# The opening of a hybrid attention layer: two tiles of x taken alone, a fixed order, and later copies

## The chip, the cores and the metric

The kernel runs on one core of one Trainium2 chip. The metric is the device time of one execution in microseconds, the median of several runs. Names used below: PE is TensorE (matmuls and transposes), DVE is VectorE, ACT is ScalarE, POOL is GpSimd, SP is the engine whose queue issues most transfers (DMAs).

## The reference

One decoder layer on x of 1024 positions by 1024 columns, in float32:

```python
def hybrid_layer(x, ...):
    h = rms_norm(x, pre_g)
    z = jnp.einsum('bsd,de->bse', h, w_in)            # 1024 x 7184 columns of weights
    qa, ka, va, ga, qb, kb, vb, gb, gk_low = split_columns(z)
    oa = diff_attention(qa, ka, va, lam)              # 8 heads, two softmax maps each, causal
    oa = rms_norm(oa, subln_g) * (1.0 - lam_init) * silu(ga)
    gk = gk_low @ w_gk_up + b_gk
    ob = gla_chunked(qb, kb, vb, log_sigmoid(gk) / 16)  # 4 heads of gated linear attention
    ob = rms_norm(ob, gla_g) * silu(gb)
    y = concatenate([oa, ob]) @ w_out
    return x + rms_norm(y, post_g)

def rms_norm(x, g):
    y = x * rsqrt(mean(x * x, axis=-1) + 1e-6)
    return y * g
```

## The kernel before

**Tiles.** x is eight tiles of 128 positions. Each is loaded, normed (`norm_x`: ScalarE squares and sums a tile, `rstd` makes the reciprocal root out of small ScalarE and VectorE steps, `scale_x` multiplies the tile by it), and turned by TensorE transposes (`tr`), 128 by 128 at a time, into PSUM banks. There are eight banks, handed out and taken back in turn by `take_bank` and `free`.

**High and low parts.** A float32 product is made of three matmuls of a faster 32-bit type: each operand is split into a rounded high part and the rest, the low part. ScalarE makes high parts, VectorE low parts: `put` for turned x (with the norm's gain `pre_g`), `make_weights` for weights (L315 and L316), `parts` for sums.

**Seven products.** The big product x by w_in is done in the Strassen-Winograd way: x and each block of weights (a "pair", 256 columns) are cut into two by two blocks, and seven products with sums of blocks replace eight. `order` lists the steps as (pair, product); one step is 24 matmuls of 256 columns for a wide pair (VA, VB), 12 of 512 for others. Products 1 and 2 need only h11 and h12, blocks of x's first four tiles; product 4 needs h22, and 5, 6, 7 and 3 need the sums s1, s2, s3 and s4. `blocks(j)` turns a quarter of the other four tiles, splits h22 and makes s1, s2 and s3; s4 is made afterwards (L625 and L627). A wide pair with an odd number uses the same weights as the even one before it, on the other two tiles of the half: in `multiply` the even pair reads tiles 0 and 1 of a half, the odd one tiles 2 and 3.

**The opening.** x's tiles 0 to 3 are loaded, then pre_g, the weights of pair 0, x's tiles 4 to 7, and more weights. `norm_x` runs for tiles 0 to 3, `first(0)` turns the first half of the columns of all four (16 transposes) and splits it into h11, step 0 runs, `first(1)` makes h12, two steps run, tiles 4 to 7 are normed, one more step runs, and then four times `blocks(j)` and a step; two steps follow, and s4.

**What sets the order.** All matmuls and transposes stay in program order (`mm` and `tr`). For the rest a scheduler lists each engine's instructions ahead of time by a simulated timeline, in program order where it can, and moves ready work ahead. `tc.keep_in_program_order` pins an instruction among the pinned ones of its engine; `tc.issue_after` puts one behind another. On the chip each engine then takes its list strictly in order. `prepare(i)` makes the weights of step i, `go(n)` runs n steps and prepares three steps ahead; weights come from buffers (`raw`, four of 512 KB) filled through SP's queue, and split weights lie in a ring of five buffers (`NRING`).

```python
        for st in range(1, NT - 1):
            part, nxt = nxt, mix(st + 1)
            rows = slice(ENDS[st - 1] * P, ENDS[st - 1] * P + P)
            sp.dma_start(out[0, rows, :], x[0, rows, :])
```

These lines, in `out_early` late in the program, copy six tiles of x to the output, onto which the result is added at the end. Nothing holds them back, so in the scheduler's list they stand early in SP's queue.

Of the kernel before, what the change touches and what calls it, by code (L numbers as in the profile page):

```python
# [14 lines left out]
P = 128  # L15
# [16 lines left out]
def hymba_kernel(  # L32
# [21 lines left out]
    act, dve, pool, pe, sp = nc.scalar, nc.vector, nc.gpsimd, nc.tensor, nc.sync  # L54
# [145 lines left out]
    order = [(0, 1), (1, 1), (0, 2), (1, 2), (2, 1), (3, 1), (2, 2), (3, 2), (4, 1), (4, 2)]  # L200
# [21 lines left out]
    LEAD = 8  # L222
    ws, ws_wide, early = {}, {}, {}

    def load_early(p):

        c0 = pairs[p][2]
        if wide(p):
# [4 lines left out]
        for kh, r in enumerate(early[p]):  # L233
            rows = slice(kh * 512, kh * 512 + 512)
            n = 256 if wide(p) else P
            sp.dma_start(r, w_in[0, rows, c0 : c0 + n].rearrange("(k p) c -> p k c", p=P))

    def prepare(i):

        if i >= len(order) or i in ws:  # L240
            return
        if i < 4:

            act_ins, dve_ins = normed[0][:2]
            with tc.issue_after(act_ins.ins), tc.issue_after(dve_ins.ins):
                make_weights(i)
        else:
            make_weights(i)
# [171 lines left out]
    def step(i):  # L420
# [22 lines left out]
        if n == 1:  # L443
            snap("s1", ps)
        elif n == 2:
            done(0, 0, ps, b["s1"])
            free.append(b["iy"])
        elif n == 6:
            snap("s2", ps)
        elif n == 7:  # L450
            snap("s3", ps)
            free.append(b["ix"])
            done(1, 1, b["z"], b["s3"])
            done(1, 0, b["y"], b["s3"])
            free.append(b["iy"])
        elif n == 3:
            done(0, 1, ps, b["s2"])
            free.append(b["iz"])
# [25 lines left out]
    norms, normed = {}, []  # L484

    def norm_x(*sts):
        n = len(sts)
        ssq = const.tile([P, 4, n], F32, tag=f"ssq{sts[0]}", name="ssq", bufs=1)
        for i, st in enumerate(sts):
            junk = hw.tile([P, D], F32, tag=("s2_hi0", "s2_lo0")[st % 2], name="junk")  # L490
            ins = act.activation(
                junk, xs[st], AF.Square, scale=D**-0.5, accum_out=ssq[:, 0, i : i + 1]
            )
            if n == 1:
                tc.keep_in_program_order(ins)
        pin = tc.keep_in_program_order if n == 1 else None
        normed[:] = [rstd(nc, ssq[:, :, :n], ssq[:, 0, :n], eps_t, pin)]
        for i, st in enumerate(sts):
            norms[st] = ssq[:, 1, i : i + 1]
            if n == 1:  # L500
                pin(scale_x(st, cols(0), dve))
# [10 lines left out]
    load_early(2)  # L512
    load_early(4)
    for st in range(4):
        norm_x(st)
    for st in range(4):
        scale_x(st, cols(1))

    def put(ps, k, dst, j):
        hi, lo = dst  # L520
        act.activation(at(hi, j), ps, AF.Copy, scale=pre_g[:, k : k + 1])
        dve.scalar_tensor_tensor(
            at(lo, j), ps, pre_g[:, k : k + 1], fp(at(hi, j)), ALU.mult, ALU.subtract
        )
# [4 lines left out]
    def first(h):  # L529

        ps = [take_bank([P, 512], "xT") for _ in range(HB)]
        for i in range(4):
            for j in range(HB):
                k = h * HB + j
                tr(ps[j][0][:, i * P : (i + 1) * P], xs[i][:, k * P : (k + 1) * P])
        hi, lo = H[("h11", "h12")[h]]
        for j in range(HB):
            put(ps[j][0], h * HB + j, (hi, lo), j)
            if h:
                act.activation(f1[h][:, j], ps[j][0], AF.Copy, scale=pre_g[:, h * HB + j : h * HB + j + 1])  # L540
            else:
                pool.tensor_tensor(f1[h][:, j], fp(at(hi, j)), fp(at(lo, j)), ALU.add)
# [51 lines left out]

    def go(n):
        for _ in range(n):
            i = made[0]
            if i == len(order):
# [23 lines left out]
    go(2)  # L622
# [89 lines left out]
    sp.dma_start(bgk, b_gk[0].rearrange("(t p) -> p t", p=P))  # L712
# [7 lines left out]
    sp.dma_start(sub_g, attn_subln_g[0].rearrange("(p o) -> p o", o=1))  # L720
    dve.tensor_scalar(sub_g, sub_g, 1.0 - LAM_INIT, None, ALU.mult)
    sp.dma_start(gla_g, gla_norm_g[0].rearrange("(t p) -> p t", p=P))
# [536 lines left out]
    def out_early():  # L1259
# [109 lines left out]
    LAST, ENDS = 2, [4, 5, 6, 7, 0, 1, 2, 3]  # L1369
# [156 lines left out]
```

## Time and profile before

| what | value |
|---|---|
| median of 3 runs | 979.72 us (978.95 to 979.96) |
| the profiled execution | 979.08 us, of which the span is 977.4 |
| granted TensorE clock, mean | 0.999 |
| busy: PE, DVE, ACT, POOL | 98%, 75%, 61%, 15% |
| first transpose, first product | 7.21 us, 14.41 us |

The span runs from the first instruction to the last; what lies around it is in the execution's time and not in the profile. A row of the timeline gives start, duration, engine, line, operation, tiles written and read, shapes and count; in brackets stands how long the engine was idle before it and what released it.

### The profile page before, as it was taken

The numbers are of one execution on the slowest core, as the hardware profiler recorded it, in microseconds if no ns is written. First come the engines' busy times: TensorE is split into PE (matmuls) and PEld (weight loads), VectorE is DVE, ScalarE is ACT, GpSimd is POOL, SyncE is SP. The second block draws the span as 40 slices with busy tenths as digits, with TensorE's granted clock in tenths as the row PEclk, the third lists the DMA queues.
The fourth block names the chain that finished last, engine by engine and source line by source line (L and its number), as shares of the span: only waits on it lengthen the run. The fifth ranks groups of instructions, "written<-read, shape, count | busy, mean of one in ns | idle before, by whom it ended". The sixth has DMA issues, their size and how long they took to land.

```text
span 977.4 us, 15766 instructions
## 1 busy us (share of the span) xinstructions
PE 956.7 (98%) x5338; PEld 830.4 (85%) x5338; DVE 735.4 (75%) x1452; ACT 600.5 (61%) x1164; POOL 142.9 (15%) x158
## 2 busy tenths in 40 slices
PE   5999999999999999999999999999999999999997
PEld 5998988888889998999888888878888888888785
DVE  6887597789866667686786876487888888898554
ACT  8742455487357455454665775366776687887773
POOL 4300000000000010000200002121322222443321
PEclk9999999999999999999999999999999999999999
DMA  9432446656774868897987866987656669994677
GB/s 345 151 110 91 139 135 205 231 179 225 238 247 162 264 187 286 254 294 229 293 259 243 273 202 191 407 269 272 197 186 228 240 199 344 340 294 105 151 208 147
DMA packets 152593, 220.45 MB, mean 226 GB/s; under 512 B 17104, under 2 KB 83664, under 8 KB 152416
## 3 DMA queue, kind: packets, MB, share of 16 engines
q1 hardware_dynamic: 146176, 203.71, 64.1%
q0 software_dynamic: 6336, 15.73, 7.0%
q8 instruction: 42, 0.69, 0.3%
q14 instruction: 39, 0.32, 0.1%
HBM read 133.93 MB, written 88.60 MB: 228 GB/s over the span
## 4 chain that ended last, share of the span: by engine, by line
PE 95%; DVE 2%; ACT 1%; DMA 1%; issue 1%; POOL 0%; SPq 0%; DVEq 0%; ACTq 0%; POOLq 0%
PE x L117 24%; PE y L117 15%; PE z L117 15%; PE ypart L117 13%; PE sc L117 7%; PE po L117 5%; PE yps L117 4%; PE wtr L120 3%; PE gpo L117 3%; PE kv L117 1%; PE gkl_ps L117 1%; PE pa L117 1%; DMA x<-in_x_dram 1%; PE xT L120 1%; DVE s_lo L548 0%
## 5 line engine op out<-in xcount | busy, mean ns | idle before, releaser
L315 ACT CAST w<-w_raw 128x512 fp32r<-128x512 f32 (+1 forms) x164 | 112.4, 688 | 94.7 <-PE y L117 44.1
L316 DVE TENSOR_TENSOR w<-w_raw,w 128x512 fp32r<-128x512 f32 (+1 forms) x164 | 126.7, 774 | 50.1 <-ACT w L315 43.3
L1049 ACT ACTIVATE p<-p,stt 128x896 f32<-128x896 f32 (+7 forms) x128 | 99.3, 777 | 36.7 <-DVE stt L1039 33.9
L427 ACT COPY s<-x 128x512 f32<-128x512 f32 x84 | 49.1, 585 | 84.4 <-PE x L117 84.3
L775 POOL TENSOR_SCALAR_AFFINE_SELECT gan<-gan 128x512 f32<-128x512 f32 x8 | 16.5, 2060 | 485.4 <-ACT gan L774 449.8
L296 DVE TENSOR_TENSOR w_raw<-w_raw 128x512 f32<-128x512 f32 (+1 forms) x96 | 75.9, 791 | 13.9 <-DMA w_raw<-in_w_in_dram 12.6
L1039 DVE CUSTOM_DVE_ANT_0 p<-sc,maskt 128x512 f32<-128x512 f32 (+3 forms) x128 | 74.3, 585 | 14.5 <-PE sc L117 13.3
L117 PE MATMUL ypart<-wo_hi,m_hi 128*128 128x512 f32 x192 | 79.5, 414 | 0.1
L117 PE MATMUL y<-h_hi,w 128*128 128x512 f32 x320 | 79.6, 391 | 0.0
L117 PE MATMUL z<-s_hi,w 128*128 128x512 f32 x320 | 79.6, 391 | 0.0
L117 PE MATMUL x<-s_hi,w 128*128 128x512 f32 x320 | 79.6, 391 | 0.0
L1055 POOL TENSOR_SCALAR p<-p,stt,lam 128x1024 f32<-128x1024 f32 (+3 forms) x64 | 56.2, 879 | 146.9 <-DVE stt L1054 141.9
L117 PE MATMUL ypart<-wo_hi,m_lo 128*128 128x512 f32 x192 | 75.5, 393 | 0.0
L117 PE MATMUL ypart<-wo_lo,m_hi 128*128 128x512 f32 x192 | 75.4, 393 | 0.0
L117 PE MATMUL sc<-k,q 128*128 128x512 f32 (+1 forms) x192 | 69.0, 363 | 1.3 <-DVE stt L1039 1.2
L117 PEld LDWEIGHTS x<-s_hi,w 128*128 128x128 f32 x320 | 59.7, 188 | 12.2
L117 PEld LDWEIGHTS y<-h_hi,w 128*128 128x128 f32 x320 | 59.6, 188 | 12.2
L117 PEld LDWEIGHTS z<-s_hi,w 128*128 128x128 f32 x320 | 59.5, 188 | 12.0
L117 PE MATMUL sc<-ks,q 128*128 128x512 f32 (+1 forms) x192 | 66.1, 347 | 0.0
L1097 ACT CAST wt_hi<-wtr 128x512 fp32r<-128x512 f32 (+1 forms) x80 | 42.7, 534 | 24.6 <-PE wtr L120 23.8
L1098 DVE TENSOR_TENSOR wt_lo<-wtr,wt_hi 128x512 fp32r<-128x512 f32 (+1 forms) x80 | 50.7, 633 | 8.6 <-ACT wt_hi L1097 8.0
L1058 DVE SCALAR_TENSOR_TENSOR p<-p,stt,p 128x1024 f32<-128x1024 f32 (+3 forms) x64 | 52.1, 814 | 4.1 <-POOL p L1055 3.9
(226 smaller groups left out, 2247.7 us busy)
## 6 DMA issues: line engine op xcount, KB each, us to landing
w_raw<-in_w_in_dram SPq DMA_DIRECT2D x56, 512.0 KB, 4.7
wo_raw<-in_w_out_dram SPq DMA_DIRECT2D x32, 256.0 KB, 3.0
wo_d<-wo_hi SPq DMA_DIRECT2D x32, 256.0 KB, 2.8
wo_d<-wo_raw SPq DMA_DIRECT2D x32, 256.0 KB, 3.8
q<-q_d SPq DMA_DIRECT2D x32, 256.0 KB, 4.7
k<-k_d SPq DMA_DIRECT2D x32, 256.0 KB, 5.7
ks<-k_d SPq DMA_DIRECT2D x64, 128.0 KB, 6.2
v<-v_d SPq DMA_DIRECT2D x16, 512.0 KB, 7.0
```

What stands on the lines that cost most here:

```text
L117: tc.keep_in_program_order(pe.matmul(*a, **k))
L120: tc.keep_in_program_order(pe.transpose(dst, src, ident))
L296: dve.tensor_tensor(dst, a, b, ALU.subtract)
L315: act.copy(w[0], src)
L316: dve.tensor_tensor(w[1], src, fp(w[0]), ALU.subtract)
L427: act.copy(b[k], ps)
L1039: ins = dve.tensor_tensor_reduce(p[:, a:e], sc[:, : e - a], maskt[:, NZ + P - (e - a) :] if last else maskt[:, : e - a], 1.0, 3e38 if i == ...
L1049: act.activation(p[:, :n], p[:, :n], AF.Exp, bias=st[:, m : m + 1], scale=-1.0, accum_out=st[:, 2 + m : 3 + m],)
L1055: pool.tensor_scalar(p1[:, :n], p1[:, :n], st[:, 5:6], lam, ALU.mult, ALU.mult)
L1058: dve.scalar_tensor_tensor(p0[:, :n], p0[:, :n], st[:, 4:5], p1[:, :n], ALU.mult, ALU.subtract)
L1097: act.copy(hi[:, :n], pt[:, :n])
L1098: dve.tensor_tensor(lo[:, :n], pt[:, :n], fp(hi[:, :n]), ALU.subtract)
```

## The change

- An engine wrapper (`Queue`) pins every ScalarE, VectorE and POOL instruction in program order while `pinned` is set, which holds from the first norm to the end of the first six steps.
- Transfers are issued as x tiles 0 and 1, the first half of pair 0's weights, pre_g, the first half of pair 2's weights, x tiles 2 and 3, the other halves, x tiles 4 to 7, and more weights.
- Tiles 0 and 1 are normed, turned and split alone (`first_tiles(0)`, half as wide); steps 0 and 1 are now (0,1) and (2,1), which read only these. Then tiles 2 and 3 follow (`first_tiles(2)`), step 2 (1,1), the second half of the columns of all four (`second_half`), step 3 (3,1), and two more steps, and only then the four rounds of `blocks(j)` and a step. The two steps behind the rounds are gone: they stand ahead of them.
- The squares of tiles 3, 5 and 7 are made by VectorE (`tensor_tensor_reduce`), not ScalarE. POOL scales the second half of the columns of tiles 0 to 3, and all of tiles 4 to 7, as before.
- The weights of step (0,5) are made behind the last pinned VectorE instruction.
- The six copies of x to the output are pinned in SP's queue at steps 20, 24, 28, 32, 36 and 40; the small loads bgk, sub_g and gla_g, and the scaling of sub_g, are pinned where the program has them.

```diff
-    act, dve, pool, pe, sp = nc.scalar, nc.vector, nc.gpsimd, nc.tensor, nc.sync
+    pe, sp = nc.tensor, nc.sync
+    pinned = [False]
+    class Queue:
...
+            def run(*a, **k):
+                ins = op(*a, **k)
+                if pinned[0]:
+                    tc.keep_in_program_order(ins)
+                    self.last = ins
+                return ins
...
+    act, dve, pool = Queue(nc.scalar), Queue(nc.vector), Queue(nc.gpsimd)
...
-    order = [(0, 1), (1, 1), (0, 2), (1, 2), (2, 1), (3, 1), (2, 2), (3, 2), (4, 1), (4, 2)]
+    order = [(0, 1), (2, 1), (1, 1), (3, 1), (0, 2), (1, 2), (2, 2), (3, 2), (4, 1), (4, 2)]
...
+    COPIES = range(20, 44, 4)
...
-        if i < 4:
-
-            act_ins, dve_ins = normed[0][:2]
-            with tc.issue_after(act_ins.ins), tc.issue_after(dve_ins.ins):
-                make_weights(i)
-        else:
+        with tc.issue_after(dve.last.ins) if order[i] == (0, 5) else nullcontext():
             make_weights(i)
...
+            if st in by_dve:
+                dve.tensor_tensor_reduce(
+                    junk, xs[st], xs[st], 1.0 / D, 0.0, ALU.mult, ALU.add, ssq[:, 0, i : i + 1]
+                )
+            else:
+                act.activation(
+                    junk, xs[st], AF.Square, scale=D**-0.5, accum_out=ssq[:, 0, i : i + 1]
+                )
...
-    for st in range(4):
+    for st in range(2):
         load_x(st)
+    load_raw(0, (0,))
     sp.dma_start(pre_g, pre_norm_g[0].rearrange("(k p) -> p k", p=P))
-    load_raw(0)
+    load_early(2, (0,))
+    for st in range(2, 4):
+        load_x(st)
+    load_raw(0, (1,))
+    load_early(2, (1,))
     for st in range(4, 8):
         load_x(st)
...
-    def first(h):
+    def first_tiles(n):
 
+        ps = [take_bank([P, 2, 256], "xT") for _ in range(2)]
+        for i in range(2):
+            for j in range(HB):
+                tr(ps[j // 2][0][:, j % 2, i * P : (i + 1) * P], xs[n + i][:, j * P : (j + 1) * P])
+        for j in range(HB):
+            put(ps[j // 2][0][:, j % 2], j, H["h11"], j, slice(n * P, n * P + 256))
...
+    def copy_x(st):
+
+        rows = slice(st * P, st * P + P)
+        tc.keep_in_program_order(sp.dma_start(out[0, rows, :], x[0, rows, :]))
+
     def go(n):
         for _ in range(n):
             i = made[0]
+            if i in COPIES:
+                copy_x(ENDS[COPIES.index(i)])
...
+    pinned[0] = True
+    norm_x(0)
+    norm_x(1)
     prepare(0)
-    first(0)
-    for i in range(1, 4):
+    first_tiles(0)
+    prepare(1)
+    norm_x(2, 3, by_dve=(3,))
+    later = []
+    step(0)
+    step(1, later)
+    first_tiles(2)
+    for snap in later:
+        snap()
...
+    whole_first(0, 1)
+    for i in range(2, 5):
         prepare(i)
-    go(1)
-    first(1)
+    norm_x(4, 5, by_dve=(5,))
+    whole_first(2, 3)
+    later.clear()
+    step(2, later)
+    xt = second_half()
+    whole(xt, 0)
+    for snap in later:
+        snap()
+    step(3)
+    made[0] = 4
+    norm_x(6, 7, by_dve=(7,))
+    whole(xt, 1, 2, 3)
     go(2)
-    norm_x(4, 5)
-    norm_x(6, 7)
-    go(1)
+    pinned[0] = False
     for j in range(HB):
         blocks(j)
         go(1)
-    go(2)
...
-            rows = slice(ENDS[st - 1] * P, ENDS[st - 1] * P + P)
-            sp.dma_start(out[0, rows, :], x[0, rows, :])
```

`whole` and `whole_first` keep the unsplit blocks f1 of x for the sums, as `first` did before; `later` only moves the copy of a product out of its bank (`snap`) behind the next splits.

More of the change, by code (lines that the diff above doesn't have):

```diff
@@ L232, in load_early @@
             early[p] = [r[:, 0], r[:, 1]]
-        for kh, r in enumerate(early[p]):
+        for kh in halves:
+            r = early[p][kh]
             rows = slice(kh * 512, kh * 512 + 512)
@@ L418, in hymba_kernel, with step @@
     sums = {}
-    def step(i):
+    def step(i, later=None):
         p, n = order[i]
@@ L441, in done @@
             take(kind, m, half, unit, c)
-        if n == 1:
+        if n == 1 and later is not None:
+            later.append(lambda: snap("s1", ps))
+        elif n == 1:
             snap("s1", ps)
@@ L482, in scale_x, with norm_x @@
         return engine.tensor_scalar(x_cs, x_cs, norms[st], 1.0, ALU.mult, ALU.mult)
-    norms, normed = {}, []
-    def norm_x(*sts):
+    norms = {}
+    def norm_x(*sts, by_dve=()):
         n = len(sts)
@@ L511, in hymba_kernel, with put, second_half @@
     load_raw(1)
-    load_early(2)
     load_early(4)
[L514 to L524, printed above, removed]
-    f1 = [hpool.tile([P, HB, 512], F32, tag=f"s4_{n}0", name=f"f1{n}") for n in ("hi", "lo")]
-    def first(h):
+    def put(ps, k, dst, j, cs=slice(0, 512)):
+        hi, lo = (at(part, j)[:, cs] for part in dst)
+        act.activation(hi, ps, AF.Copy, scale=pre_g[:, k : k + 1])
+        dve.scalar_tensor_tensor(lo, ps, pre_g[:, k : k + 1], fp(hi), ALU.mult, ALU.subtract)
+    f1 = [hpool.tile([P, HB, 512], F32, tag=f"s4_{n}0", name=f"f1{n}") for n in ("hi", "lo")]
+    def first_tiles(n):
[5 more added lines that the diff above has]
+            put(ps[j // 2][0][:, j % 2], j, H["h11"], j, slice(n * P, n * P + 256))
+        for _, i in ps:
+            free.append(i)
+    def second_half():
         ps = [take_bank([P, 512], "xT") for _ in range(HB)]
@@ L533, in first, with whole @@
             for j in range(HB):
-                k = h * HB + j
+                k = HB + j
                 tr(ps[j][0][:, i * P : (i + 1) * P], xs[i][:, k * P : (k + 1) * P])
-        hi, lo = H[("h11", "h12")[h]]
         for j in range(HB):
[L538 to L542, printed above, removed]
+            put(ps[j][0], HB + j, H["h12"], j)
+        return ps
+    def whole(ps, *js):
+        for j in js:
+            k = HB + j
+            act.activation(f1[1][:, j], ps[j][0], AF.Copy, scale=pre_g[:, k : k + 1])
             free.append(ps[j][1])
@@ L1367, in hymba_kernel @@
     opened.update(dict.fromkeys(Y))
[L1369 removed]
+    LAST = 2
     def open_bank(b):
```

37 lines of the change are left out of this document (22 added, 15 removed).

## Prediction

> **What bounds the kernel now.** I read the page first: its busy line, and the shares of the chain that ended last.
>
> ```profile
> span 977.4 us, 15766 instructions
> PE 956.7 (98%) x5338; PEld 830.4 (85%) x5338; DVE 735.4 (75%) x1452; ACT 600.5 (61%) x1164; POOL 142.9 (15%) x158
> PE 95%; DVE 2%; ACT 1%; DMA 1%; issue 1%; POOL 0%; SPq 0%; DVEq 0%; ACTq 0%; POOLq 0%
> ```
>
> TensorE holds 95% of the chain. An average hides stages, so next comes the table by windows (start:end, length; then busy time and count for PE, PEld, DVE, ACT, POOL; then granted clock, DMA share, GB/s).
>
> ```profile
> 0.00:5.00 5.00, 0.00 (x0) 0.00 (x0) 0.00 (x0) 1.92 (x2) 1.83 (x11) 1.00 0.59 213
> 5.00:10.00 5.00, 2.20 (x8) 1.43 (x8) 2.37 (x9) 4.11 (x13) 1.82 (x2) 1.00 1.02 314
> 10.00:15.00 5.00, 2.82 (x10) 1.95 (x11) 4.28 (x9) 4.84 (x10) 1.85 (x2) 1.00 1.05 389
> 35.00:60.00 25.00, 23.58 (x175) 22.21 (x174) 24.84 (x38) 16.25 (x26) 1.70 (x2) 1.00 0.12 37
> 60.00:80.00 20.00, 19.32 (x148) 17.79 (x148) 17.03 (x26) 7.85 (x12) 0.00 (x0) 1.00 0.50 141
> 80.00:400.00 320.00, 320.00 (x1797) 280.14 (x1796) 239.28 (x374) 171.51 (x290) 6.77 (x4) 1.00 0.63 203
> ```
>
> From 80 to 400 us TensorE never rests: what the opening 60 us save or lose is handed on to the end. TensorE misses 10.0 of the first 15 us and 1.4 from 35 to 60, where VectorE is full (24.84 of 25). So two bounds meet in this change: the start, and VectorE at 35 to 60. The timeline of the start follows, one row per run of alike instructions (start, duration, engine, line, operation).
>
> ```profile
> 0.81 1.81 SPq L477 DMA_DIRECT2D x<-in_x_dram  x4
> 4.37 1.06 ACT L491 ACTIVATE junk<-x 128x1024 f32<-128x1024 f32 x1 [2.28 <-DMA x<-in_x_dram]
> 8.38 1.06 ACT L491 ACTIVATE junk<-x 128x1024 f32<-128x1024 f32 x1 [0.63 <-DMA x<-in_x_dram]
> 8.76 1.12 PE L120 MATMUL xT<-ident,x 128*128 128x128 f32 x4 [0.47 <-DVE x L482]
> 11.60 2.17 ACT L315 CAST w<-w_raw 128x1024 fp32r<-128x1024 f32 x2
> 13.68 2.42 ACT L521 ACTIVATE h_hi<-xT,pre_g 128x512 fp32r<-128x512 f32 x4
> 14.41 4.24 PE L117 MATMUL x<-w,h_hi 128*128 128x256 f32 x16 [0.58 <-ACT h_hi L521]
> 18.45 1.72 PE L117 MATMUL x<-w,h_lo 128*128 128x256 f32 x8
> 20.01 1.91 PE L120 MATMUL xT<-ident,x 128*128 128x128 f32 x16
> 24.63 2.08 PE L117 MATMUL y<-w,h_hi 128*128 128x256 f32 x16
> 27.51 2.08 PE L117 MATMUL y<-w,h_hi 128*128 128x256 f32 x16
> ```
>
> The third x tile is what ScalarE waits for until 8.38; the first product starts at 14.41, after four tiles are normed and turned. The products of one step, 24 matmuls, take 5.6 us the first time (14.41 to 20.01) and 2.88 later (24.63 to 27.51): a slow start of 2.7 us, though the clock column says 1.00 throughout. The later rows of TensorE:
>
> ```profile
> 41.63 1.04 PE L120 MATMUL xT<-ident,xt 128*128 128x128 f32 x8
> 43.98 2.15 PE L117 MATMUL y<-w,h_hi 128*128 128x256 f32 x16 [1.32 <-DVE s L565]
> 52.40 2.08 PE L117 MATMUL z<-w,s_hi 128*128 128x256 f32 x16
> 58.15 2.44 PE L117 MATMUL x<-w,s_hi 128*128 128x256 f32 x16
> 64.27 2.08 PE L117 MATMUL y<-w,h_hi 128*128 128x256 f32 x16
> 67.15 2.08 PE L117 MATMUL x<-w,s_hi 128*128 128x256 f32 x16
> ```
>
> A product has waited 1.32 us for a PSUM bank that VectorE (L565) still read. 52.40 is product (0,5), the first that needs sums of all eight x tiles: my finish line for the opening.
>
> **The change part by part: TensorE's timetable.** (1) *First product.* Weights of pair 0 now come as third transfer in SP's queue, where the third x tile was, and that one was there at 8.38. Casting 1024 columns takes 1.08 (2.17 for two): 9.46. The x tiles 0 and 1 are ready in time: tile 1 was being turned from 8.76, with four transposes in 1.12. The split of the transposed tile needs pre_g.
>
> ```profile
> pre_g<-in_pre_norm_g_dram SPq DMA_DIRECT2D x1, 4.0 KB, 7.4
> out_dram<-in_x_dram SPq DMA_DIRECT2D x6, 512.0 KB, 7.5
> bgk<-in_b_gk_dram SPq DMA_DIRECT2D x1, 2.0 KB, 7.5
> ```
>
> pre_g lands 7.4 us after its issue (the number that ends these rows); behind three transfers, at 0.45 us of SP each (1.81 for four), it is issued at 2.2 and there at 9.6. From the first split to the first product were 0.73 us for 512 columns (13.68 to 14.41); for 256 I estimate 0.5. First product: 10.1, 4.3 earlier. Bounds: 9.5 and 11.5, should the two weight transfers among the x tiles slow each other.
>
> (2) *Slow start.* As before, 5.6 us for step 0: it ends at 15.7. Step 1 is (2,1), also on tiles 0 and 1, at 2.88: 18.6. Its weights are the fourth transfer, its cast lies behind the splits on ScalarE: beside step 0. By the Trainium skill, TensorE: Matmul & The Clock Gate, "Part 1: The HAM clock gate", the array runs at half rate until about 3.4 us of activity fill a window that runs freely; the factor two of the rows agrees, the page's clock event does not show here. By it the slow stretch may be 3.4 to 6.8 us, and the sum would shift by about 1 us either way.
>
> (3) *Tiles 2 and 3.* They are now the fifth and sixth of 512 KB. The windows' rates give 2.63 MB by 10 us, so 3.15 MB by 11.3; the third, 1.57 MB, was moved by 6.6 and seen at 8.38, so add 1.8: 13.1. A square (1.06 plus its read), norm and scaling took from 4.37 to 8.7 for two tiles one after the other; here the two run on two engines: about 17. TensorE comes at 18.6, so this is hidden with 1.6 to spare; if the transfer is later by more, all of it shows. Then 8 transposes, 0.9 (half of the row of 16), and a new wait: step 2 needs their splits, and four half splits at about 0.4 feed 8 matmuls that take 0.12 each. First split 0.5, then 1.6 against 0.96: +1.2, bounds 0.4 and 2. Step 2 ends at 23.6, 16 transposes 25.4, steps 3, 4, 5 at 34.0.
>
> (4) *Tiles 4 to 7.* blocks(0) needs all four scaled by POOL. Behind the splits of tiles 2 and 3 (about 21) POOL has f1hi and the scaling:
>
> ```profile
> 16.17 5.99 POOL L542 TENSOR_TENSOR f1hi<-h_hi,h_lo 128x512 f32<-128x512 f32 x4 [2.95 <-DVE h_lo L522]
> 24.42 5.41 POOL L482 TENSOR_SCALAR xt<-xt,ssq 128x1024 f32<-128x1024 f32 x4 [2.25 <-ACT h_hi L521]
> ```
>
> 5.99 and 5.41 make 32.4 without a gap. But pinned order puts a wait ahead: the low part of the weights of (0,2) needs a sixth buffer of a ring of five, free only when step 2 ends (23.6); queued behind it on VectorE are the square of tile 5, that norm, and the low parts of the second half, for which step 4 waits (two thirds into it, from 28.3). That delays POOL up to 2: 34.4. Against 34.0 the wait is 0 to 2, I take 0.5. (5) *Blocks.* Four times 8 transposes (0.87) and one step (2.88) make 15.0: (0,5) starts at 49.5. Two steps fewer lie behind the blocks, and each step now takes a bank that was filled one block earlier, so the 1.32 wait goes. Sum: 52.4 − 49.5 = 2.9 us gained (−4.3 start, +0.9 eight more transposes after it, +1.2, +0.5, −1.3, roundings).
>
> (6) *VectorE*, which is full there:
>
> ```profile
> 19.14 1.88 DVE L296 TENSOR_TENSOR w_raw<-w_raw 128x1024 f32<-128x1024 f32 x1 [0.42 <-DMA w_raw<-in_w_in_dram]
> 20.95 1.24 DVE L1482 TENSOR_SCALAR ssq<-ssq,eps_t 128x2 f32<-128x2 f32 x1
> 22.17 1.21 DVE L296 TENSOR_TENSOR w_raw<-w_raw 128x1024 f32<-128x1024 f32 x1
> 36.66 0.74 DVE L522 SCALAR_TENSOR_TENSOR h_lo<-xT,pre_g,h_hi 128x512 fp32r<-128x512 f32 x1
> 37.32 0.74 DVE L565 SCALAR_TENSOR_TENSOR s<-xT,pre_g,h 128x512 f32<-128x512 f32 x1
> 37.98 0.68 DVE L316 TENSOR_TENSOR w<-w_early,w 128x512 fp32r<-128x512 f32 x1
> 58.09 1.22 DVE L316 TENSOR_TENSOR w<-w_raw,w 128x1024 fp32r<-128x1024 f32 x1
> 64.58 1.23 DVE L316 TENSOR_TENSOR w<-w_raw,w 128x1024 fp32r<-128x1024 f32 x1
> 66.30 1.23 DVE L296 TENSOR_TENSOR w_raw<-w_raw 128x1024 f32<-128x1024 f32 x1 [0.50 <-DMA w_raw<-in_w_in_dram]
> ```
>
> It gets three squares of 1024 columns (1.21 each by the row at 22.17: +3.6), and the subtractions at 19.14 and 22.17, done early so far, come behind the pinned phase (+2.4 there). The pinned low parts of the second half end about 29.5; behind them a square 1.2, its norm 1.0, the low parts of (2,2) and (4,1) 1.8 and two sums 1.2 make it free at 34.7. It then owes until the low part of (0,7): blocks 4 × (2 × 0.66 + 5 × 0.60) = 17.3, subtractions and low parts of (0,5), (0,6), (0,4), (0,7) 8 × 1.14 = 9.1, sums and one weight 3.0, the difference block s4 4.8: 34.2, ending at 68.9, against 65.8 in the row at 64.58. TensorE wants that part a third into (0,7): 68.1 so far, 65.2 if 2.9 are gained. Only if s4 (wanted much later, by (0,3)) goes behind it, 64.1, does VectorE keep up. I take 0, bounds 0 and +3.7. (7) *Moved transfers.* Six copies of x, 7.5 us to landing, leave the opening and enter SP's queue at steps 20 to 40, ahead of raw weights; bgk, sub_g and gla_g stay behind the opening instead of in it. Weights are made three steps ahead, 8.6 us, which covers a copy: 0, up to +1 each without that cover.
>
> So 979.08 (the profiled execution; 977.4 of span, 1.7 around it) − 2.9 = 976.2; the median 979.72 lies 0.6 above it: **976.8 us**.
>
> **The rivals.** *A, no new waits*: splits and POOL keep ahead of TensorE; 1.2 + 0.5 are not lost: 975.1. For it: ScalarE gives up three squares; against it: 8 matmuls take less than their splits.
>
> *B, VectorE hands the gain back*: low parts in program order, s4 first. (0,7) then starts near 68.9 − 0.96 = 67.9 against 67.15; with some of s4 deferred it is level: 979.5, within the bound. For it: the row 35 to 60, full now, and s4 sums that the order of today puts between the blocks; against it: only 2.4 of the 4.8 must move.
>
> *C, slower: VectorE and POOL block each other.* The subtraction of 1024 columns took 1.88 beside f1hi and 1.21 after it, and a norm of two columns 1.24 beside it; POOL's 11.4 us now fall on five large VectorE operations with two SBUF inputs (two squares, three low parts), 0.67 each: 3.3 on top of B's 68.9, (0,7) at 71.3, up to 4.1 late; with half of s4 deferred 2.9 late: 982.6. It decides from the point where the low part of (0,7) ends after 70.1 (68.1 + 2.0). The Trainium skill, SBUF — State Buffer, "Who interferes with whom", says that such a pair takes turns on a shared port for a whole instruction; the 1.88 agrees; by it the sum is C's.
>
> *D, a copy ahead of raw weights* stalls a step at 85 to 145 us, six times the 1 us of (7): 976.8 + 6 = 982.8. Against it: windows from 80 on show no idle at all. *E, the start isn't earlier* since x and w share the engines of DMA: part of B's result.
>
> **How the numbers follow.** Two runs of this kernel differ by up to 0.1% (978.95 to 979.96), so 0.2%, 2.0 us, is about what can be told. Forecast 0.42, A 0.13, B with E 0.25, C 0.15, D 0.05. The forecast's own range is 975.5 to 978.3; with A and B and most of C it is 974.5 to 981.3. Faster 0.55, same 0.25, slower 0.20 (C and D).
>
> **What would show it.** First product at 10.1 with weights, not x, as the third arrival; 24 matmuls of 5 to 6 us, then a wait of about 1 us for h_hi ahead of step 2; blocks(0) near 34; (0,5) near 49.5. The forecast is wrong if (0,7) waits for a low part, if VectorE's subtraction or squares show 1.5 us or more, or if TensorE shows idle between 80 and 145 us.

## The result and the profile after

The changed kernel takes 1002.22 us (median of 5, 1000.34 to 1003.15) against 979.72 (978.87 to 980.1) of the kernel before on the same chip: ratio 1.0228, 95% interval 1.0217 to 1.024. It is 22.5 us slower; the prediction said 976.8 with a range to 981.3. The page of the changed kernel, with span, busy line and the chain's shares:

```profile
span 1000.5 us, 15773 instructions
PE 973.3 (97%) x5338; PEld 832.8 (83%) x5338; DVE 740.5 (74%) x1460; ACT 600.3 (60%) x1160; POOL 138.1 (14%) x158
PE 87%; DVE 5%; DMA 2%; ACT 2%; issue 2%; SPq 1%; POOL 0%; DVEq 0%; ACTq 0%; POOLq 0%
```

TensorE's share of the chain fell from 95 to 87%, and VectorE and ScalarE rose. But TensorE's *busy* time rose as well, from 956.7 to 973.3 us, with the same 5338 matmuls. So the matmuls themselves took longer: in part, as it turns out, at a lower clock in the opening, in part at full clock all through the kernel. The windows (columns as in the prediction) say where the clock was lost:

```profile
20.00:24.00 4.00, 2.58 (x17) 1.86 (x16) 1.75 (x4) 2.22 (x6) 2.27 (x2) 1.00 1.11 341
24.00:26.00 2.00, 2.00 (x12) 2.00 (x11) 0.18 (x2) 2.00 (x4) 0.24 (x1) 0.51 0.36 86
26.00:28.00 2.00, 2.00 (x14) 2.00 (x13) 2.00 (x2) 0.04 (x1) 0.00 (x0) 0.64 0.00 0
54.00:60.00 6.00, 4.02 (x10) 3.18 (x11) 6.00 (x9) 2.85 (x4) 0.00 (x0) 0.56 0.00 0
60.00:66.00 6.00, 3.92 (x20) 3.43 (x19) 6.00 (x11) 3.30 (x5) 0.00 (x0) 0.78 0.28 87
80.00:400.00 320.00, 319.32 (x1799) 274.57 (x1798) 236.82 (x373) 165.76 (x278) 2.60 (x3) 1.00 0.64 203
```

The granted clock (third column from the right) falls to 0.51 and 0.56 in or right behind stretches in which TensorE paused. TensorE's timeline of the opening (an operation's line is now 137 or 140 for TensorE and 66 for the wrapped engines, so tiles identify it):

```profile
10.03 0.80 PE L137 MATMUL x<-w,h_hi 128*128 128x256 f32 x2
16.73 2.28 PE L137 MATMUL x<-w,h_hi 128*128 128x256 f32 x16
19.80 1.04 PE L140 MATMUL xT<-ident,x 128*128 128x128 f32 x8
21.18 0.50 PE L137 MATMUL x<-w,h_hi 128*128 128x256 f32 x2 [0.35 <-ACT h_hi L66]
22.21 0.87 PE L137 MATMUL x<-w,h_hi 128*128 128x256 f32 x4 [0.53 <-ACT h_hi L66]
23.62 2.19 PE L137 MATMUL x<-w,h_hi 128*128 128x256 f32 x10 [0.55 <-ACT h_hi L66]
25.61 1.91 PE L137 MATMUL x<-w,h_lo 128*128 128x256 f32 x8
27.32 1.98 PE L140 MATMUL xT<-ident,x 128*128 128x128 f32 x16
38.45 1.04 PE L140 MATMUL xT<-ident,xt 128*128 128x128 f32 x8
55.98 3.75 PE L137 MATMUL y<-h_hi,w 128*128 128x512 f32 x8 [3.66 <-DVE s L66]
61.24 1.02 PE L137 MATMUL z<-w,s_hi 128*128 128x256 f32 x6
64.35 2.00 PE L137 MATMUL z<-w,s_hi 128*128 128x256 f32 x10 [2.08 <-ACT s_hi L66]
70.97 2.06 PE L137 MATMUL x<-w,s_hi 128*128 128x256 f32 x16
79.49 2.06 PE L137 MATMUL x<-w,s_hi 128*128 128x256 f32 x16
```

The start is 4.4 us earlier than before (10.03 against 14.41). But the blocks begin at 38.45, (0,5) starts at 61.24 where it was 52.40, and (0,7) at 79.49 where it was 67.15: the opening ends 12.3 us *late*. TensorE hardly stands still after that (busy 319.32 of 320 us from 80 on). So nearly all of the other 10 us must lie in matmuls that run one behind the other. Three rows of the changed kernel's timeline near 300 us:

```profile
298.93 2.03 PE L137 MATMUL x<-s_hi,w 128*128 128x512 f32 x8
300.79 1.09 PE L137 MATMUL x<-s_lo,w 128*128 128x512 f32 x4
301.73 2.03 PE L137 MATMUL x<-h_hi,w 128*128 128x512 f32 x8
```

and of the kernel before:

```profile
300.92 1.98 PE L117 MATMUL x<-s_hi,w 128*128 128x512 f32 x8
302.73 1.07 PE L117 MATMUL x<-s_lo,w 128*128 128x512 f32 x4
303.64 1.98 PE L117 MATMUL y<-h_hi,w 128*128 128x512 f32 x8
```

From start to start a step of twelve matmuls with 512 columns takes 2.80 us instead of 2.72 at a granted clock of 1.00 in both. There are 140 such steps: 11.2 us. Steps of 24 matmuls with 256 columns became a little faster (70.97 to 73.81 is 2.84; 2.88 before), 56 of them: 2.2 back. That leaves 9.0 of the 10 us; after 80 us TensorE also waits once for VectorE for 1.1 us, which the kernel before does not.

The list of buffer addresses in the two built programs suggests why. The change needs one small tile of constants fewer (tiles 2 and 3 share one), and such a small tile takes 32 bytes. The buffers allocated behind them, the ring of weights among them, moved down by 32 bytes (61952 to 61920), while the blocks of x, allocated from the other end, stayed (h11's high part at 146944). So the two operands of those matmuls, the weights and a block of x, stand 32 bytes differently to each other. The first experiments test this.

### The profile page after: what moved, and what is told of

Same layout as the page of the kernel before. It is cut to its first block, busy times and chain, and to the rows that moved or that the text cites. A ratio compares the mean times of both kernels' runs of the same rounds, so it can differ in the third digit from the quotient of the medians.

```text
span 1000.5 us, 15773 instructions
## 1 busy us (share of the span) xinstructions
PE 973.3 (97%) x5338; PEld 832.8 (83%) x5338; DVE 740.5 (74%) x1460; ACT 600.3 (60%) x1160; POOL 138.1 (14%) x158
## 4 chain that ended last, share of the span: by engine, by line
PE 87%; DVE 5%; DMA 2%; ACT 2%; issue 2%; SPq 1%; POOL 0%; DVEq 0%; ACTq 0%; POOLq 0%
PE x L137 21%; PE z L137 14%; PE y L137 14%; PE ypart L137 13%; PE sc L137 7%; PE po L137 5%; PE yps L137 4%; PE wtr L140 3%; PE gpo L137 2%; PE kv L137 1%; DVE c L66 1%; PE gkl_ps L137 1%; DVE h_lo L66 1%; DVE w L66 1%; DMA w_raw<-in_w_in_dram 1%
## 5 line engine op out<-in xcount | busy, mean ns | idle before, releaser
L137 PE MATMUL y<-h_hi,w 128*128 128x512 f32 x320 | 83.3, 403 | 3.7 <-DVE s L66 3.7
L66 POOL TENSOR_SCALAR_AFFINE_SELECT gan<-gan 128x512 f32<-128x512 f32 x8 | 13.1, 1640 | 497.5 <-ACT gan L66 497.5
L66 DVE TENSOR_TENSOR c<-z,s 128x512 f32<-128x512 f32 x48 | 33.1, 689 | 32.2 <-ACT s L66 18.6
```

The source lines that it names most:

```text
L66: ins = op(*a, **k)
L137: tc.keep_in_program_order(pe.matmul(*a, **k))
```

## The experiments

Each run stands beside the kernel before on the same chip. "Above before" is the difference of the two medians, and the "base" of a run is the kernel that it was made from. Each changed kernel was run four times and its times spread over 1 to 4 us, so a difference of 1 to 2 us between two changed kernels is not clear of noise.

**The place of the buffers (three runs).** The changed kernel with 32 bytes of padding, nothing else:

```diff
-    eps_t = const.tile([P, 1], F32, name="eps_t")
+    eps_t = const.tile([P, 9], F32, name="eps_t")[:, :1]
```

> The changed kernel with 32 bytes more in the pool of constants, so that the weight buffers start at a multiple of 64 bytes again, as before the change; every engine's instruction order is that of the changed kernel. Theory 1 (the address): the steps of 12 matmuls of 512 columns go back from 2.80 to 2.72 us, those of 24 matmuls of 256 from 2.84 to 2.88, and the time falls by 8 to 11 us, to about 992; the opening stays as it is, (0,5) at about 61 us. Rival (the moved copies, or the order): the address does nothing, the steps stay at 2.80 and the time at 1002.

Measured: 992.31, ratio 1.0122 (1.0105 to 1.0138), 12.5 above before: 10 of the 22.5 us are gone. The step with 512 columns is back at 2.72:

```profile
304.93 1.98 PE L137 MATMUL z<-s_hi,w 128*128 128x512 f32 x8
306.75 1.07 PE L137 MATMUL z<-s_lo,w 128*128 128x512 f32 x4
307.65 0.83 PE L137 MATMUL gpo<-gan,gv 128*128 128x128 f32 x6
```

The opening stayed (its (0,5) at 61.39). Next the reverse: the kernel *before*, with its weights 32 and its blocks of x 64 bytes higher; then with both 32 bytes higher (112 in place of 104).

```diff
+    eps_t = const.tile([P, 9], F32, name="eps_t")[:, :1]
-    pool.memset(edge.tile([P, 120], F32, name="edge"), 0.0)
+    pool.memset(edge.tile([P, 104], F32, name="edge"), 0.0)
```

> The kernel before with its weight buffers moved by 32 bytes and x's blocks by 64, instruction order unchanged. Theory 1: 512-column steps at 2.80 us instead of 2.72, and 8 to 11 us slower than before, about 989. Rival: same as before, 979.7 within 1.

Measured: 990.01, ratio 1.0101 (1.0085 to 1.0118). The kernel before loses 10.2 us with the same instructions in the same order. Its rows give 2.80 (305.50 to 308.30), at a clock that is 1.00 as before:

```profile
305.50 2.03 PE L117 MATMUL x<-s_hi,w 128*128 128x512 f32 x8
307.37 1.09 PE L117 MATMUL x<-s_lo,w 128*128 128x512 f32 x4
308.30 2.03 PE L117 MATMUL y<-h_hi,w 128*128 128x512 f32 x8
```

> The kernel before with the weight buffers and x's blocks both moved by 32 bytes, order unchanged. If what counts is where the two operands of a matmul lie to each other, as before: 979.7 within 1. If what counts is the weight buffer's own address, about 989. If each operand off a multiple of 64 costs by itself, more than 989.

Measured: 981.22, ratio 1.0017 (1.0008 to 1.0026), with steps of 2.72 (301.62 to 304.34). Both operands were moved and the pace stayed: it is the place of the two to each other that counts. The median is still 1.4 above before. That is not in the pace; the profiled execution has a wait of 1.9 us for VectorE, and I did not trace it further. A try to use this for a gain gave the buffers of the wide weights (256 columns) a shift of 32 bytes inside slots of 4160:

```diff
-    w = [ap.tile([P, HB, 256], F32R, tag="ring", name="w", bufs=NRING) for _ in range(2)]
+    w = [ap.tile([P, HB * 256 + 16], F32R, tag="ring", name="w", bufs=NRING)[:, 8 : 8 + HB * 256]
+         .rearrange("p (k c) -> p k c", c=256) for _ in range(2)]
...
```

> The kernel before with the weights of the wide pairs (256 columns moving past x's blocks) 32 bytes into their buffers, those of the others at a multiple of 64 as before; instruction order unchanged. Theory 1 in detail (32 bytes between the two operands slow 512 moving columns and speed 256 moving ones): wide steps at 2.84 instead of 2.88 us, 56 of them, so 2 us faster: 977.5. Rival (the wide steps' gain in the shifted runs had another cause): same as before.

Measured: 985.96, ratio 1.0065 (1.005 to 1.008), a miss. The wide steps did come down from 2.88 to 2.85. But slots of 4160 bytes put three of the five narrow weight buffers (512 columns) 64 bytes off the blocks modulo 128, and most of their steps took 2.80. Of the two buffers with equal places modulo 128 one gave steps of 2.72 to 2.76, the other of 2.78 to 2.80. So equal places alone are not enough for the fast pace, and whether 64 bytes off is slow by itself, this run does not separate.

**The moved copies.** The kernel before with the six copies of x pinned at steps 20 to 40 as in the change:

```diff
+            if i in COPIES:
+                copy_x(ENDS[COPIES.index(i)])
...
-            sp.dma_start(out[0, rows, :], x[0, rows, :])
...
```

> The kernel before with the six copies of x moved to steps 20 to 40 and nothing else. Theory: no effect within 1 us (979.7), since no step from 80 us on waits for weights. Rival: raw weights behind the copies come late and cost 1 us a copy, up to 6 us.

Measured: 979.96, ratio 1.000 (0.9991 to 1.0009). No cost of the copies can be told.

**The shared banks.** From here on every kernel has the 32 bytes of padding, so that only the opening differs. ScalarE's and VectorE's rows of the changed kernel around step 2:

```profile
20.65 0.47 ACT L66 ACTIVATE h_hi<-xT,pre_g 128x256 fp32r<-128x256 f32 x1 [3.10 <-PE xT L140]
21.68 0.84 ACT L66 ACTIVATE h_hi<-xT,pre_g 128x256 fp32r<-128x256 f32 x2 [0.55 <-DVE h_lo L66]
23.10 0.47 ACT L66 ACTIVATE h_hi<-xT,pre_g 128x256 fp32r<-128x256 f32 x1 [0.58 <-DVE h_lo L66]
```

```profile
21.16 0.48 DVE L66 SCALAR_TENSOR_TENSOR h_lo<-xT,pre_g,h_hi 128x256 fp32r<-128x256 f32 x1 [2.58 <-ACT h_hi L66]
22.19 0.88 DVE L66 SCALAR_TENSOR_TENSOR h_lo<-xT,pre_g,h_hi 128x256 fp32r<-128x256 f32 x2 [0.54 <-ACT h_hi L66]
23.61 0.48 DVE L66 SCALAR_TENSOR_TENSOR h_lo<-xT,pre_g,h_hi 128x256 fp32r<-128x256 f32 x1 [0.54 <-ACT h_hi L66]
```

ScalarE's split of a quarter waits for VectorE's split of the quarter before, and the reverse: two quarters share a bank, and the engines take turns on it. Four splits last 3.4 us (20.65 to 24.09) instead of some 1.7. The Trainium skill, PSUM — Partial Sum Buffer, "PSUM bank collisions raise a hardware error", says that the scheduler of the compiler's back end adds a dependency between instructions of different engines on one bank and quadrant, reads among them; these rows agree. The experiment gives each quarter its own bank:

```diff
-        ps = [take_bank([P, 2, 256], "xT") for _ in range(2)]
+        ps = [take_bank([P, 256], "xT") for _ in range(HB)]
...
```

> As the first of these runs, and each quarter of the turned tiles 0 and 1, and 2 and 3, in a PSUM bank of its own (four banks of 256 columns instead of two of 512). Theory 2 (ScalarE and VectorE take turns on a bank): splits no longer alternate, the four take 1.7 us instead of 3.5, step 2 does not fall to half rate, and the opening gains 2 to 4 us on the first of these runs. Rival (VectorE's list is the bound in the opening): step 2 is earlier, but (0,5) and all behind it stay within 1 us.

Measured: 989.86, ratio 1.01 (1.0083 to 1.0117): 2.4 us less than with the padding alone, by the medians (the single times, 988.93 to 991.51 against 990.61 to 993.39, overlap), and 10 above before. The rows of TensorE:

```profile
19.24 2.56 PE L137 MATMUL x<-w,h_hi 128*128 128x256 f32 x16 [0.23 <-ACT h_hi L66]
34.73 1.03 PE L140 MATMUL xT<-ident,xt 128*128 128x128 f32 x8
52.23 3.56 PE L137 MATMUL y<-h_hi,w 128*128 128x512 f32 x8 [3.65 <-DVE s L66]
66.76 2.08 PE L137 MATMUL x<-w,s_hi 128*128 128x256 f32 x16
```

Step 2 runs through at a clock of 1.00, and the blocks begin at 34.73, 3.7 us earlier and close to the 34.0 of the prediction. With the padding alone (0,6) started at 71.11, so that in these two executions 4.35 us arrive there. Yet 3.65 us of waiting for VectorE stay. The steps (0,5) and (0,6) are still 4.2 and 8.6 us behind those of before (56.64 against 52.40, 66.76 against 58.15).

**What holds VectorE up.** Squares back on ScalarE (`by_dve` dropped), on top of the own banks:

> As the run with a bank for each quarter, and the squares of tiles 3, 5 and 7 on ScalarE again. Theory 3 (VectorE has too much in the opening): VectorE is free of pinned work 2 to 4 us earlier, the waits for VectorE at the last blocks (3.7 and 3.1 us) shrink, and the time falls by 2 to 4 us, to about 987. Rival (the order of VectorE's list, not its load): the waits move with it, less than 1 us is gained; ScalarE, with 3.5 us more in the pinned order, may even cost 1 to 2.

Measured: 988.53, ratio 1.0094 (1.0079 to 1.0109), 8.8 above before. The 1.3 us between the two are not clear of noise, and the wait of 3.65 stayed as it was. Next, still with own banks alone, `blocks` does only what reads PSUM and returns the rest, which runs one round later, so that banks are emptied first:

```diff
+        return lambda: rest(j, h21, s1)
...
-        blocks(j)
+        rests.append(blocks(j))
+        if j:
+            rests.pop(0)()
...
```

> As the run with a bank for each quarter, and in each round of blocks(j) only what empties the PSUM banks is written ahead of the step (the turned block's copy, its split and its sum with the other half); high and low parts and differences of the sums follow one round later. Theory 4 (order of VectorE's list): no product waits for a bank behind VectorE any more (3.7 us now), TensorE keeps full rate, (0,5) starts near 50 instead of 56.6, and the time falls by 3 to 6 us, to 984 to 987. Rival (load): (0,5) comes earlier but waits there for its sums, and less than 1.5 us is gained.

Measured: 989.14, ratio 1.0101 (1.0084 to 1.0118), 9.4 above before where the base was 10.0 above: no gain that can be told. But the written order hardly reached VectorE's own list: the sum of the third block, for which TensorE waits 3.65 us here too, ran 17.5 us behind the low part of the weights that opens the stretch, as in the base (33.05 and 50.55; 33.82 and 51.34). So this run does not decide whether the order within the blocks matters. Next, on the kernel with own banks and squares on ScalarE (988.53), two ways to loosen the first phase: the blocks after five steps instead of six, and the fixed order taken off.

```diff
-    norm_x(4, 5)
+    norm_x(4, 5); norm_x(6, 7)
...
-    norm_x(6, 7)
     whole(xt, 1, 2, 3)
-    go(2)
+    go(1)
     pinned[0] = False
     for j in range(HB):
         blocks(j)
         go(1)
+    go(1)
```

and, in the other kernel,

```diff
-                    tc.keep_in_program_order(ins)
...
-        rstd(nc, ssq[:, :, :n], ssq[:, 0, :n], eps_t, tc.keep_in_program_order if pinned[0] else None)
+        rstd(nc, ssq[:, :, :n], ssq[:, 0, :n], eps_t, None)
```

> Base: the changed kernel with the 32 bytes of padding, own banks for the quarters, squares on ScalarE (988.53). One thing moved: the blocks of tiles 4 to 7 begin after five steps instead of six (the step (0,2) ahead of them, (1,2) between them), for which the norms of tiles 6 and 7 stand right behind those of 4 and 5, and the fixed order ends one step earlier. Theory (the order is what is left of the loss: VectorE idles in the fixed phase, 27.8 to 33.7 with two short breaks, and starts the blocks at 38.5 instead of 32.3): its first block product (h_lo 128x512 behind the tiles 4 to 7) comes at 32 to 34, the wait of 3.65 us for s is under 1, (0,5) starts at 50 to 52 instead of 55.7, and the time is 983, within 1.5. Rival (VectorE is full whatever the order, since the two subtractions of raw weights and the squares' share stay where they are): (0,5) not before 54.5, time 987 or more.

> Same base (988.53). Only the fixed order is taken off ScalarE, VectorE and GpSimd in the first phase; all steps and transfers stay. Theory (where the blocks stand costs, not that the order is fixed): within 1.5 us of 988.5, (0,5) at 55 to 57. Rival (the fixed order itself keeps VectorE idle and pushes the subtractions of raw weights into the blocks): VectorE fills the idle stretch of 28 to 33 with subtractions, (0,5) at 52 or earlier, time 985 or less.

Measured: 989.23 (1.0098, 1.0083 to 1.0113) and 988.44 (1.0092, 1.0075 to 1.0109): neither gains. My theory of the blocks' place fell in its time. In that run (989.23) VectorE's first product of the blocks came at 35.87 instead of 38.48, the wait for s fell from 3.65 to 0.51 and 0.95, and (0,5) started at 52.75, between what the theory and its rival gave. But 2.58 for f1lo came ahead, 2.54 for s_hi and 1.95 for s_lo behind, and (0,6) started at 67.08. Of this some 2.2 us are clock: the step ahead of it took 5.10 us (61.98 to 67.08), at a granted clock of 0.50. The run without fixed order came out as its theory had it, (0,5) at 54.96 and the time unchanged. In both runs VectorE is busy to 65 or later without a gap of note.

What all of these share is that the change lets weights (0,5) wait for the last pinned VectorE instruction. Two subtractions of raw weights, which ran at 19.14 and 22.17 before, now stand inside VectorE's full stretch. That wait taken away, on each of the two:

```diff
-        with tc.issue_after(dve.last.ins) if order[i] == (0, 5) else nullcontext():
+        with nullcontext():
```

> Base: the kernel of the late-blocks experiment (989.23), where VectorE is busy without a gap from 32.4 to 65, of that 4 x 1.14 us for subtractions of raw weights. One thing taken away: weights (0,5) no longer wait for the last instruction of the fixed phase, so that the first two subtractions stand ahead of the splits of the second half. Theory (what is left is work of VectorE that the change pushed from the idle opening into the full stretch): two subtractions at 21 to 26, the stretch shorter by 2.3, the low part of the weights (0,6) at 63.3 instead of 65.6, time 986.5 to 987.5. Rival (TensorE's own waits for f1lo and banks, 2.58 and 2.54 us, set the end): within 0.7 of 989.2.

> Base: the kernel without fixed order (988.44), where VectorE still did no subtraction of raw weights before 38.0 since weights (0,5) wait for the last instruction of the first phase. That wait taken away too. Theory (this wait, not the fixed order, pushes the subtractions into the full stretch): the two subtractions at 19 to 26, (0,5) 2 to 3 us earlier than 54.96 or its wait of 4.66 for s_hi shorter by as much, time 985.5 to 986.5. Rival: within 0.7 of 988.4.

Measured: 987.58 beside 980.97 of before (1.007, 1.0046 to 1.0094), 6.6 above it where its base was 9.5 above; and 990.14 beside the same (1.0101, 1.0071 to 1.013), 9.2 above where its base was 8.7 above. The first came out at the time expected, and its subtractions stand early:

```profile
23.56 1.21 DVE L66 TENSOR_TENSOR w_raw<-w_raw 128x1024 f32<-128x1024 f32 x1
25.10 1.22 DVE L66 TENSOR_TENSOR w_raw<-w_raw 128x1024 f32<-128x1024 f32 x1
```

The way there was only in part the expected one. The low part of (0,6) came at 64.61, 1.0 earlier and not 2.3. (0,6) itself started 2.73 earlier (64.35), but 2.2 of that is the step ahead of it, which took 2.87 us (61.48 to 64.35) at a clock of 1.00 where its base had 5.10 at 0.50. So the 2.9 us between the two runs are not the price of the two subtractions alone, and what these cost is not shown. The second was a miss: without fixed order the subtractions went (22.54 and 25.53) ahead of splits that TensorE waited for, and the second half's transposes began at 27.92 instead of 26.35.

**The load itself.** Twelve VectorE subtractions (the low parts of s2, s3 and s4, 0.60 us each, 7.2 together) left out, with zeros from GpSimd in their place: once in the changed kernel with own banks and squares on ScalarE, once in the kernel before.

```diff
-        dve.tensor_tensor(at(lo, j), f, fp(at(hi, j)), ALU.subtract)
+        dve.tensor_tensor(at(lo, j), f, fp(at(hi, j)), ALU.subtract) if n == "s1" else pool.memset(fp(at(lo, j)), 0.0)
```

> Base: the changed kernel with padding, own banks and squares on ScalarE (988.53). Left out: the low parts of the blocks s2, s3 and s4 (twelve VectorE subtractions of 128x512, 0.60 each, 7.2 us in the stretch of 38 to 68); GpSimd writes zeros there instead, and TensorE multiplies as before. Theory (VectorE's load in the stretch is what is left of the opening's loss): the waits of 3.65 for s and 3.09 for s_hi shrink to under 2 together, the step (0,6) starts at 60 to 62 instead of 66.28, time 981 to 984. Rival (TensorE's own start, its clock and the banks): waits stay, time over 986.5.

> The kernel before with the same twelve subtractions left out (zeros by GpSimd instead). Theory: before, VectorE is full too but TensorE waits for it only 1.32 and 0.68 us up to the step at 70.87, so at most 1 to 2 us are gained: 977.7 to 979. If it gains as much as the changed kernel does (5 or more), VectorE's load is no difference between the two and the theory falls.

Measured: 984.9 (1.0051, 1.0033 to 1.0068), 5.0 above before where the base was 8.8 above; and 980.36 for the kernel before (1.0003, 0.9993 to 1.0012), no gain. So the same load on VectorE costs the changed kernel 3.8 us and the kernel before nothing that can be told. The first gained less than I had expected (981 to 984). The waits of TensorE from 10 to 80 us in the run of 984.9 (total, times, longest):

```profile
PE y L137 <- DVE s L66: 2.6, 1, 2.6
PE xT L140 <- POOL xt L66: 1.3, 1, 1.3
PE z L137 <- ACT s_hi L66: 1.2, 1, 1.2
PE y L137 <- ACT f1lo L66: 1.0, 1, 1.0
```

The two expected to vanish are 2.6 and 1.2 now (3.9 and 3.1 with the low parts), and 2.3 us of others stand ahead of them: 1.3 for GpSimd's scaling, which is new, and 1.0 for f1lo, which was there before. At last the four subtractions for s4 on GpSimd, nothing left out, in the kernel before and in the one of 987.58:

```diff
-        dve.tensor_tensor(s4[j // 2][:, j % 2], f1[1][:, j], f1[0][:, j], ALU.subtract)
+        pool.tensor_tensor(s4[j // 2][:, j % 2], f1[1][:, j], f1[0][:, j], ALU.subtract)
```

> The kernel before with the four subtractions for s4 on GpSimd instead of VectorE (4 x 0.60 less for VectorE in 44 to 60; 4 x 1.28 by the f1hi row for GpSimd, which is idle there). Nothing left out. Gain at most the waits of 1.32 and 0.68: 978 to 979.5. Against it: a VectorE subtraction beside a GpSimd operation took 1.88 instead of 1.21, four such give 2.7 back to VectorE: no change, within 0.6 of 979.7.

> Base: late blocks and early subtractions (987.58 beside 980.97 of before, 6.6 above it). The four subtractions for s4 on GpSimd instead of VectorE, nothing left out. Theory (VectorE is the bound of 34 to 64): 1.5 to 2.4 less, 4 to 5 above before; with the shared stretches lengthened by GpSimd, as 1.88 against 1.21 showed: no gain. Rival (TensorE's waits for f1lo, 3.0, and for its clock): no gain either, but then without longer VectorE operations in the trace.

Measured: 981.33 (1.0013, 1.0004 to 1.0023), and 987.55 beside 979.92 (1.0079, 1.0064 to 1.0094), 7.6 above where its base was 6.6 above. Neither gains; the kernel before even loses 1.4. There, four VectorE operations beside GpSimd's four became longer, together by 2.9 us, where GpSimd had taken over 2.4; two of them:

```profile
43.71 1.77 DVE L548 TENSOR_TENSOR s_lo<-f1hi,s_hi 128x512 fp32r<-128x512 f32 x1
56.33 1.72 DVE L296 TENSOR_TENSOR w_raw<-w_raw 128x1024 f32<-128x1024 f32 x1
```

The same operations take 0.68 and 1.21 alone. There, what GpSimd takes off VectorE it gives back as a slower VectorE. In the run of 987.55 four VectorE operations became longer too, by 3.2, but the clock had a share: 16 matmuls took 3.28 and 3.37 us (from 29.73 and 61.57) where its base had 2.17 and 2.07.

No version here beats the kernel before.

## Why the prediction was wrong, point by point

**Nowhere in the text: the place of the buffers, 10 us.** Some 10 of the 22.5 us were in no step and in no rival. I priced instructions and waits, and took the pace of a matmul as a constant. That the place costs this is shown by three runs: padding takes 9.9 us off the changed kernel (1002.22 to 992.31), the same shift costs the kernel before 10.2, and a shift of both operands leaves the pace alone. Why the place matters stays open.

**(1) First product at 10.1: right in the number,** 10.03, but in part by luck. Weights were the third arrival, as I said. But pre_g landed some 5.8 us after its issue, at 8.0 instead of 9.6, and the first split waited for the transposes instead.

**(2) Slow start: off by 1.0.** Step 0 ended at 16.73, not 15.7, as the splits that feed it took turns on a bank; with own banks it ended at 15.10.

**(3) Tiles 2 and 3: the wait was right, its consequence was missed.** I gave 1.2 us for splits slower than matmuls; the rows give 0.35 + 0.53 + 0.55 = 1.43. But I had counted four splits of 0.4 in a row, not two engines taking turns on a bank, and not that TensorE's pauses lower the clock: step 2 took 6.1 us (21.18 to 27.32), of which 1.1 are waits and 2.9 work; the other 2.2 go with a clock of 0.51 and 0.64. The sum had step 2 end at 23.6. Own banks left 0.23 of the waits and none of the clock's loss, and the blocks then began at 34.73 against 34.0 forecast.

**(4) POOL: right in its size,** 0 instead of 0.5 at 38.45, but with no room: GpSimd's last scaling ended at 38.46. In the run of 984.9, where TensorE came earlier, it waited 1.25 us for GpSimd.

**(5) Blocks in 15.0 us: the step that failed most.** They took 22.8 (38.45 to 61.24). I argued that the wait of 1.32 for a bank goes, since a step takes a bank filled one block earlier. It became 3.66, because VectorE, which empties the bank, was further behind than before. With two smaller waits (0.80 and 0.29) that is 4.75 of the 7.8 us too many. Another 2.6 are clock: the step behind that wait took 5.3 us (55.98 to 61.24) instead of 2.7, at a clock of 0.56.

**(6) VectorE: load right, consequence wrong.** I forecast 34.2 us of work from 34.7 on, to the low part of (0,7). The same work took 34.5 us here, so the load was right. But it began at 41.26, 6.6 late, and ended at 78.10 (the last row here), with 1.2 us of waits and a further subtraction of 1.1 inside. Of the 6.6, 2.95 were there when the pinned low parts ended (32.45). The rest is a square and a low part, costed at some 1.2 each and run beside GpSimd (the first two rows), a norm longer by 0.7, and a wait of 1.51 for ScalarE's high part of the same weights:

```profile
32.37 1.87 DVE L66 CUSTOM_DVE_ANT_0 junk<-xt 128x1024 f32<-128x1024 f32 x1
37.57 1.96 DVE L66 TENSOR_TENSOR w<-w_early,w 128x1024 fp32r<-128x1024 f32 x1 [1.51 <-ACT w L66]
55.10 0.74 DVE L66 SCALAR_TENSOR_TENSOR s<-xT,pre_g,h 128x512 f32<-128x512 f32 x1
62.90 0.74 DVE L66 SCALAR_TENSOR_TENSOR s<-xT,pre_g,h 128x512 f32<-128x512 f32 x1
76.88 1.22 DVE L66 TENSOR_TENSOR w<-w_raw,w 128x1024 fp32r<-128x1024 f32 x1
```

Above all I asked only when the stretch *ends*, for the weights of (0,7), and allowed s4 to be put off. That end was not what held TensorE: (0,7) starts at 79.49 without a wait. TensorE was held by operations in the middle of the queue: the sum of the third block at 55.10, which frees its bank, and that of the fourth at 62.90, for (0,5). I took 0 with bounds to +3.7; with banks and padding out of the way, 10.0 us of loss against before remained. Of that, leaving out the twelve low parts takes 3.8, and this is shown. The squares' 1.3 are not clear of noise, and the 2.9 between the runs without and with early subtractions are in good part clock. These are not separate shares, since all act on the same queue. What is left with banks, squares and low parts out of the way, 5.0, stands as waits for f1lo, xt, s and s_hi; I did not take it apart further, and its cause stays open.

**(7) Copies at 0: right,** 979.96 against 979.78.

**The rivals.** A did not occur: TensorE waited 1.43 us for the splits in step 2 alone. B had the right place with far too small a price, for the reason in (6). C's mechanism is in the rows (1.87 and 1.96 beside GpSimd), but these two rows are only 1.4 us longer, and the norm's first small step 0.8 (1.06 instead of 0.23); that is a small part of the 10.0 lost there. D did not occur, and neither did E: TensorE waits for no transfer after 80 us, and the start was 4.4 earlier. That the pinned order itself would be to blame, as I came to think, did not hold: without it no change of the time could be told.

## What to carry to other kernels

An engine that is full is not priced by when its work ends but by when each result in the middle comes that another engine waits for; work that ran in an idle opening and is pushed behind a fixed phase can come back as waits there. If a profile shows the same matmuls with more busy time, compare the step time in a stretch without waits before looking at order: a constant tile added or dropped can move a whole group of buffers, and one run with a pad of 32 bytes tells whether that is it. Two engines that read neighbouring parts of a PSUM bank take turns; where they should run side by side, give each part its bank.

## What the hardware showed that I had not expected

- **The place of a matmul's two operands to each other changes its pace.** With equal places modulo 128 bytes, twelve float32 matmuls with 512 columns take 2.72 us in the kernel before and in two runs with padding or shift; 32 bytes off, 2.80. For 24 matmuls with 256 columns it is the reverse: 2.88 with equal places, 2.84 at 32 off. The granted clock is 1.00 in all. Equal places are not the whole rule: in the run of 985.96 one buffer with an equal place gave 2.78 to 2.80. Why is open.
- **Short pauses lower the clock.** In the window of 20 to 24 us TensorE was busy 2.58 of 4, with no pause over 0.55 us, and the clock was 0.51 in the next two. With own banks, and hardly a pause there, it stayed 1.00. The Trainium skill, TensorE: Matmul & The Clock Gate, "Part 1: The HAM clock gate", names an idle window of about 3.4 us as what makes it cold; the 3.66 before 55.98 fits, the short ones here do not fit such a rule for whole pauses. Eight transposes ran between the pauses, too; whether they count as work for the clock, no run here shows. Nor is the length of a single pause enough to tell: behind 3.00 us of waiting 16 matmuls took 2.17 (run of 987.58, at 30.60), behind 3.01 they took 3.28 (run of 987.55, at 29.73).
